# Twenty of the 72 blocks made ahead as split halves, expert numbers written whole, a tile's numbers turned later: a decoder block on one core

## The chip, the core and the metric

The kernel runs on one core of a Trainium2 chip. The metric is the device time of one execution in microseconds (us); lower is better. The core's engines work side by side, each through its own instructions in order: TensorE (PE; its weight loads are PEld), VectorE (DVE), ScalarE (ACT), GpSimd (POOL) and SyncE (SP), which here only issues DMA transfers.

## The reference

One decoder block on 512 tokens of width 1024, in float32:

```python
h = rms_norm(x, norm1_g);  proj = h @ w_in
y_a = hgrn2_mixer(...);  y_b = dilated_attention_mixer(...)
x = x + (sigmoid(ga) * (y_a @ w_branch_a) + sigmoid(gb) * (y_b @ w_branch_b)) @ w_out
x = x + peer_ffn(rms_norm(x, norm2_g), peer_wq, peer_subkeys, peer_u, peer_v)
```

`peer_ffn` has 16384 experts. Each of 8 heads scores two tables of 128 keys, takes the best 16 of each, and of their sums the best 16; an expert's number is 128 times the first key's index plus the second's. A token's 128 experts give `gelu(u[expert] . x) * gate`, with which the rows `v[expert]` are summed.

## The kernel before

The tokens are four tiles of 128. A first "front" (mixers, projections, queries) runs for tile 0, a second for tiles 1 to 3. The experts are then computed in two ways at once.

*By rows.* For the first product tiles 0 and 3 (`UG`), and for the second product tile 3, fetch the chosen rows of `u` or `v` one by one with indirect DMAs from POOL (`row`, L642, into the tiles `rq`, `rowx` and `row`) and sum them on DVE (L661, L684). The list of rows is `idx`, 32-bit integers.

*By blocks.* For tiles 1 and 2 (`UD`, 256 tokens) every one of the 128 blocks of 128 experts is multiplied (`hidden`, L811): the block `ub` comes over SP's queue, TensorE multiplies it with the tokens into `ph` in PSUM, and ACT writes the GELU of it to `pre` (L829; from block 56 on the same thing is written into tiles that are called `rq` and `keys_sb`). For tiles 1, 2 and 0 (`VD`) the second product goes by blocks as well, with the gates as a dense matrix `Gc`. That matrix is made by `scatter_steps`: from a token's expert numbers in two parts (`pk`, first and second key) and its weights (`pkw`), DVE writes `e1` and `e2` (both `e` in the rows, L704 and L707), ACT or DVE `eg` (L711, L713), TensorE multiplies them (`pg`, L718) and ACT writes `Gx` (L719). A step is 16 tokens: 16 products `pg`, in four groups.

The stage "ahead" (L842) makes the first 72 blocks (`NPRE`) before the main loop, since the gates of the dense tiles aren't there yet. Here `hidden` multiplies whole float32 blocks with the whole tokens `h32` (eight products, 16 instructions on TensorE). In the main loop it first splits a block: `halves` (L97) lets ACT write a rounded part `uh` and DVE the rest `ul`, both in a buffer of their own (`bufs=1`), and TensorE makes `uh` by `hH`, `uh` by `hL` and `ul` by `hH`, 24 products. In the stage ahead run also the routing of tile 3, and that of tiles 1 and 2, called when block 12 and block 30 come up (`ROUTE1`, `ROUTE2`); a routing's scatter steps are added to a pump that gives one step at every second block, and another pump gives 0.6 rows of tile 3 a block. A row's DMA and its sum wait for the GELU of the block they were called behind.

A routing (L549) takes top 16 on DVE, and then for each head `eq` (DVE, L597), `sel` and its halving (POOL, L599 and L601) and a sum that leaves the 16 expert numbers (DVE, L602):

```python
nc.vector.tensor_reduce(out=idf[:, n], in_=..., axis=AX.X, op=ALU.add)
if T in UG:
    nc.vector.tensor_copy(idx[:, UG.index(T), hn], idf[:, n])
...
nc.vector.tensor_copy(full[:, hs], idff)
```

At its end (L616 on), for a tile in `VD`, the numbers in `full` are taken apart on DVE into `i12` (its tile is called `ssb`), turned by TensorE (L624) and written to `pk`; the gates are turned by L627 to `pkw`. The main loop has for each of the 128 blocks 18 products (`acc`, L883) of `vh`, `vl` with `ah`, `al`, which ACT and DVE split from a block of `v` and from the gates, and makes blocks 72 to 127 of `hidden` on its way.

A scheduler sets the order of each engine's instructions from the order of the program, the waits and its own model of times; the engines then follow that order.

Of the kernel before, what the change touches and what calls it, by code (L numbers as in the profile page):

```python
# [8 lines left out]
F32 = mybir.dt.float32  # L9
# [5 lines left out]
ALU = mybir.AluOpType  # L15
AX = mybir.AxisListType
PSUM = bass.MemoryType.PSUM

P = 128
# [10 lines left out]
TOPK = 16  # L30
# [9 lines left out]
UG = (0, 3)  # L40
UD = (1, 2)
VD = (1, 2, 0)
# [8 lines left out]

NPRE, RING = 72, 56

ROUTE1, ROUTE2, SCAT_H = 12, 30, 2

GS = 4
ACTW = {0: (0, 4, 8, 12), 1: (0, 4, 8, 12), 2: (4, 12)}
# [16 lines left out]
def kernel(ctx: ExitStack, tc: tile.TileContext, x, wst, par, cst, cols, g2, keys, u, v, ut, vr, out):  # L74
    nc = tc.nc
# [470 lines left out]
        pt = pvg.tile([P, 512], F32, name="vg") if T and bank[0] % 2 else pr.tile([P, 512], F32, name="pr")  # L546
        return pt.rearrange("p (n k) -> p n k", k=NKEY)

    def routing(T, rq):  # L549


        gate = gates[:, T]
        full = rt.tile([P, P], F32, name="full")
        sv = rt.tile([P, PH, TOPK], F32, name="sv")
        for b in range(0, PH, 4):
            tv = rt.tile([P, 4, 2, TOPK], F32, name="tv")
            ti = rt.tile([P, 4, 2, TOPK], U32, name="ti")
            for f in range(2):
                pt = route_bank(T)
                for n in range(4):  # L560
                    nc.tensor.matmul(pt[:, n], rq[64 * f:64 * f + 64, b + n],
                                     keys_sb[64 * f:64 * f + 64, b + n], start=True, stop=True)
                ssb = rt.tile([P, 4, NKEY], F32, name="ssb")
                nc.scalar.activation(ssb, pt, AF.Copy)
                for n in range(4):
                    top16(tv[:, n, f], ti[:, n, f], ssb[:, n])
            tf = rt.tile([P, 4, 2, TOPK], F32, name="tf")
            nc.vector.tensor_copy(tf, ti)
            nc.vector.tensor_scalar(tf[:, :, 0], tf[:, :, 0], float(NKEY), None, op0=ALU.mult)
            cs = rt.tile([P, 4, NCAND], F32, name="cs")  # L570
            ci = rt.tile([P, 4, NCAND], F32, name="ci")
            for src, dst in ((tv, cs), (tf, ci)):
                off = a = 0
                while a < TOPK:
                    n = RUNS[a]
                    e = a
                    while e < TOPK and RUNS[e] == n:
                        e += 1
                    r = e - a
                    o = dst[:, :, off:off + r * n].rearrange("p h (r n) -> p h r n", n=n)  # L580
                    nc.vector.tensor_tensor(out=o, in0=src[:, :, 1, None, :n].to_broadcast([P, 4, r, n]),
                                            in1=src[:, :, 0, a:e, None].to_broadcast([P, 4, r, n]), op=ALU.add)
                    off += r * n
                    a = e
            svb = sv[:, b:b + 4]
            si = rt.tile([P, 4, TOPK], U32, name="si")
            sf = rt.tile([P, 4, TOPK], BF16, name="sf")
            idf = rt.tile([P, 4, TOPK], F32, name="idf")
            shp = [P, NCAND, TOPK]
            by_few = lambda t: t.rearrange("p c (a b) -> p c a b", b=GS)  # L590
            for n in range(4):
                top16(svb[:, n], si[:, n], cs[:, n])
            nc.vector.tensor_copy(sf, si)
            for n in range(4):
                eq = rt.tile(shp, BF16, name="eq")
                sel = rt.tile(shp, F32, name="sel", bufs=2)
                nc.vector.tensor_tensor(out=by_few(eq), in0=iota[:, :NCAND, None, :].to_broadcast([P, NCAND, TOPK // GS, GS]),  # L597
                                        in1=by_few(sf[:, n, None, :].to_broadcast(shp)), op=ALU.is_equal)
                nc.gpsimd.tensor_tensor(out=sel, in0=eq, in1=ci[:, n, :, None].to_broadcast(shp), op=ALU.mult)  # L599
                hc = NCAND // 2  # L600
                nc.gpsimd.tensor_add(sel[:, :hc], sel[:, :hc], sel[:, hc:])  # L601
                nc.vector.tensor_reduce(out=idf[:, n], in_=sel[:, :hc].rearrange("p c k -> p k c"), axis=AX.X, op=ALU.add)  # L602
                if T in UG:
                    hn = slice((b + n) * TOPK, (b + n + 1) * TOPK)
                    nc.vector.tensor_copy(idx[:, UG.index(T), hn], idf[:, n])
            hs = slice(b * TOPK, (b + 4) * TOPK)
            idff = idf.rearrange("p h k -> p (h k)")
            nc.vector.tensor_copy(full[:, hs], idff)
        gt = gate.rearrange("p (h k) -> p h k", k=TOPK)
        gs = rt.tile([P, 2, PH], F32, name="gs")  # L610
        nc.vector.tensor_tensor(out=gt, in0=sv, in1=sv[:, :, 0:1].to_broadcast([P, PH, TOPK]), op=ALU.subtract)
        nc.scalar.activation(gt, gt, AF.Exp)
        nc.vector.tensor_reduce(out=gs[:, 0], in_=gt, axis=AX.X, op=ALU.add)
        nc.vector.reciprocal(gs[:, 1], gs[:, 0])
        nc.vector.tensor_tensor(out=gt, in0=gt, in1=gs[:, 1, :, None].to_broadcast([P, PH, TOPK]), op=ALU.mult)
        if T in VD:  # L616
            pt = route_bank(T)
            i12 = rt.tile([P, 4, NKEY], F32, name="ssb")

            nc.vector.tensor_scalar(i12[:, 0], full, 1.0 / NKEY, -63.5 / NKEY, op0=ALU.mult, op1=ALU.add)  # L620
            nc.vector.tensor_scalar(i12[:, 0], i12[:, 0], RND, RND, op0=ALU.add, op1=ALU.subtract)
            nc.vector.scalar_tensor_tensor(i12[:, 1], i12[:, 0], -float(NKEY), full, op0=ALU.mult, op1=ALU.add)
            for j in range(2):
                nc.tensor.transpose(pt[:, 1 + j], i12[:, j], ident)  # L624
            nc.vector.tensor_copy(pk[:, VD.index(T), 0:2], pt[:, 1:3])
            if T in UD:
                nc.tensor.transpose(pt[:, 3], gate, ident)  # L627
                nc.vector.tensor_copy(pkw[:, VD.index(T)], pt[:, 3])

# [114 lines left out]
    rows, scat = Pump(), Pump()  # L746
# [30 lines left out]
    idx = gat.tile([P, len(UG), P], I32, name="idx", bufs=1)  # L777
# [8 lines left out]
    rt = rctx.enter_context(tc.tile_pool(name="rt", bufs=1, side="left", **TILE))  # L786
# [5 lines left out]

    f = Front(tuple(range(1, 4)), True, background)
    routing(0, rq0)
    rows.add(u_steps(UG[0]))
    mixers(f)
    rows(2 * P)
    rq1, rq2, rq3 = f.post()
# [12 lines left out]
    def hidden(b, pool):  # L811
        if RING <= b < NPRE:

            if (b - RING) % 4 == 0:
                pre4[0] = rq_pool.tile([P, 4, NU], F32, name="rq") if b - RING < 12 else rq_pool.tile([P, 4, NU], F32, name="keys_sb", bufs=1)
            dst = pre4[0][:, (b - RING) % 4]
        else:
            dst = dp.tile([P, NU], F32, name="pre", bufs=RING)
        pre.append(dst)
        ub = us.tile([P, KC, P], F32, name="ub")  # L820
        nc.sync.dma_start(out=ub, in_=ut[b].rearrange("p (k i) -> p k i", k=KC))
        pt = pool.tile([P, NU], F32, name="ph")
        if b < NPRE:

            accumulate(pt, [ub[:, k] for k in range(KC)], h32, slice(None), True)
        else:
            ubs = halves(us.tile([P, KC, P], F32R, name="uh", bufs=1), us.tile([P, KC, P], F32R, name="ul", bufs=1), ub)
            accumulate(pt, [tuple(a[:, k] for a in ubs) for k in range(KC)], (hH, hL), slice(None), True)
        return nc.scalar.activation(dst, pt, AF.Gelu)  # L829

    with tc.tile_pool(name="hw", bufs=1, side="right", **TILE) as hw, \
            tc.tile_pool(name="gb", bufs=1, side="left", **TILE) as gb, \
            tc.tile_pool(name="php", bufs=3, space=PSUM, side="right") as php, \
            tc.tile_pool(name="pg", bufs=3, space=PSUM, side="right") as pg:
        pg_bank = lambda: pg.tile([P, 512], F32, name="pg")
        h32 = hw.tile([P, KC, NU], F32, name="h32")
        nc.vector.tensor_tensor(out=h32, in0=hH.bitcast(F32), in1=hL.bitcast(F32), op=ALU.add)
        scat.add(scatter_steps(0, pg_bank))
        routing(3, rq3)
        rows.add(u_steps(3))  # L840
        lag[0] = 1
        for b in range(NPRE):  # L842
            if b == ROUTE1:
                routing(1, rq1)
                scat.add(scatter_steps(1, pg_bank))
            if b == ROUTE2:
                routing(2, rq2)
                scat.add(scatter_steps(2, pg_bank))
            behind[:] = [hidden(b, php)]
            rows(ROWS_H)  # L850
            if b % SCAT_H == 0:
                scat(1)
        scat(P)
# [103 lines left out]
```

## Time and profile before

| | |
|---|---|
| median of three runs | 1765.86 us (1764.51 to 1772.72) |
| the profiled execution | 1764.48 us, of which the span is 1762.6 us |
| TensorE busy | 1627.5 us (92%), mean granted clock 0.967 |
| VectorE busy | 1321.0 us (75%) |
| ScalarE busy | 735.6 us (42%) |
| GpSimd busy | 672.2 us (38%) |
| moved by DMA | 473.42 MB, 269 GB/s on average |

The profile is one execution. A busy share is an average over stages that have different limits, so each stage is looked at by itself. A matmul's recorded time is longer than the distance to the next one, as they overlap: how fast TensorE goes is read from the distance of the starts, or from the time of a row that merges many.

### The profile page before, as it was taken

Reading aid. Unit: us, or ns where it says so; the run is one execution under the profiler, and the core shown is the slowest. Engines: PE = TensorE matmul, PEld = TensorE weight load, DVE = VectorE, ACT = ScalarE, POOL = GpSimd, SP = SyncE. Lnnn points to the kernel's source line nnn. Section 1 sums busy time; section 2 is a strip of 40 time slices with the busy share of each in tenths; the row PEclk is TensorE's granted clock in tenths of the full one; section 3 lists DMA queues with packets and bytes.
Section 4 is the critical chain, followed back from the end, with each engine's and each line's share of the span. In section 5 each row is a group of like instructions: output and inputs, shape, how many; then the busy total and the mean of one; then the engine's idle time right before and its main releaser. Section 6 shows DMA issues by size and latency. Waiting matters only on the chain.

```text
span 1762.6 us, 26949 instructions
## 1 busy us (share of the span) xinstructions
PE 1627.5 (92%) x9725; PEld 1437.8 (82%) x9725; DVE 1321.0 (75%) x2773; ACT 735.6 (42%) x1411; POOL 672.2 (38%) x502
## 2 busy tenths in 40 slices
PE   7998969789978798998999989999999999999997
PEld 7887969678868797787889977888888878888886
DVE  2113999998988649987985566878788877887887
ACT  3323443334334556633675543333334333343332
POOL 0000366676542004353442224433344454454452
PEclk9999979889989899998999989999999999999999
DMA  8777368879885336575667789999899999898888
GB/s 290 233 231 239 120 225 281 267 275 321 308 305 199 120 120 223 175 248 162 226 223 247 262 268 341 328 321 341 323 326 344 335 322 337 323 333 314 304 303 281
DMA packets 173813, 473.42 MB, mean 269 GB/s; under 512 B 14832, under 2 KB 62192, under 8 KB 173680
## 3 DMA queue, kind: packets, MB, share of 16 engines
q1 hardware_dynamic: 116272, 268.47, 44.6%
q0 software_dynamic: 55296, 201.35, 32.0%
q10 hardware_dynamic: 2112, 1.88, 0.3%
q8 instruction: 77, 1.26, 0.3%
q14 instruction: 56, 0.46, 0.1%
HBM read 442.80 MB, written 27.79 MB: 267 GB/s over the span
## 4 chain that ended last, share of the span: by engine, by line
PE 45%; DVE 22%; DMA 20%; issue 7%; POOL 3%; ACT 2%; DVEq 0%; ACTq 0%; POOLq 0%; SPq 0%
PE acc L883 16%; PE pp L112 15%; PE ph L112 10%; DMA Gc<-g_d 8%; DMA w<-in_wst_dram 3%; DVE e L704 2%; PE pg L718 2%; DVE rq L661 2%; DVE h2g L684 2%; DMA row<-in_u_dram,idx 2%; DMA rowx<-in_u_dram,idx 2%; DMA row<-in_v_dram,idx 1%; DVE wl L99 1%; DVE row L661 1%; DMA rowx<-in_v_dram,idx 1%
## 5 line engine op out<-in xcount | busy, mean ns | idle before, releaser
L112 PE MATMUL ph<-h,ub 128*128 128x256 f32 x1152 | 263.7, 384 | 0.5 <-ACT pre L829 0.5
L883 PE MATMUL acc<-vl,ah 128*128 128x512 f32 x768 | 240.9, 395 | 8.7 <-DVE vl L879 8.7
L112 PEld LDWEIGHTS ph<-h,ub 128*128 128x128 f32 x1152 | 216.7, 193 | 29.4 <-ACT pre L829 0.9
L883 PE MATMUL acc<-vh,al 128*128 128x512 f32 x768 | 239.0, 392 | 0.0
L883 PE MATMUL acc<-vh,ah 128*128 128x512 f32 x768 | 221.1, 392 | 3.8 <-ACT vh L877 3.8
L642 POOL DMA_INDIRECT rowx<-in_u_dram,idx x96 | 131.9, 1374 | 227.7 <-ACT pre L829 56.8
L642 POOL DMA_INDIRECT rowx<-in_v_dram,idx x96 | 148.3, 1545 | 158.5 <-DVE h2g L684 65.8
L98 ACT ACTIVATE ah<-Gc 128x384 fp32r<-128x384 f32 x128 | 67.0, 524 | 309.0 <-PE acc L883 303.7
L883 PEld LDWEIGHTS acc<-vl,ah 128*128 128x128 f32 x768 | 142.7, 189 | 43.4 <-DVE vl L879 14.4
L883 PEld LDWEIGHTS acc<-vh,al 128*128 128x128 f32 x768 | 145.2, 189 | 31.5
L883 PEld LDWEIGHTS acc<-vh,ah 128*128 128x128 f32 x768 | 139.6, 188 | 30.0 <-ACT vh L877 4.4
L879 DVE TENSOR_TENSOR vl<-vb,vh 128x1024 fp32r<-128x1024 f32 x128 | 156.3, 1221 | 9.0 <-ACT vh L877 8.4
L877 ACT ACTIVATE vh<-vb 128x1024 fp32r<-128x1024 f32 x128 | 135.9, 1062 | 57.4 <-DMA vb<-in_vr_dram 56.6
L642 POOL DMA_INDIRECT rq<-in_u_dram,idx x96 | 120.2, 1252 | 88.7 <-DVE rq L661 52.1
L98 ACT ACTIVATE wh<-w 128x512 fp32r<-128x512 f32 x144 | 88.8, 628 | 132.6 <-PE pp L112 60.0
L661 DVE SCALAR_TENSOR_TENSOR rowx<-rowx,h2g 128x1024 f32<-128x1024 f32 x96 | 120.1, 1253 | 30.3 <-DMA rowx<-in_u_dram,idx 19.6
L661 DVE SCALAR_TENSOR_TENSOR rq<-rq,h2g 128x1024 f32<-128x1024 f32 x96 | 131.2, 1370 | 15.0 <-DMA rq<-in_u_dram,idx 15.0
L112 PE MATMUL ph<-hH,ul 128*128 128x256 f32 x448 | 128.4, 287 | 8.8 <-DVE ul L99 8.8
L684 DVE SCALAR_TENSOR_TENSOR h2g<-rowx,hid,h2g 128x1024 f32<-128x1024 f32 x95 | 121.7, 1281 | 18.5 <-DMA rowx<-in_v_dram,idx 18.4
L112 PE MATMUL ph<-hH,uh 128*128 128x256 f32 x448 | 128.1, 286 | 3.7 <-ACT pre L829 3.7
L112 PE MATMUL ph<-hL,uh 128*128 128x256 f32 x448 | 128.1, 286 | 0.0
L719 ACT ACTIVATE Gx<-pg 128x512 f32<-128x512 f32 x96 | 98.2, 1057 | 66.0 <-PE pg L718 59.2
(289 smaller groups left out, 3635.8 us busy)
## 6 DMA issues: line engine op xcount, KB each, us to landing
ub<-in_ut_dram SPq DMA_DIRECT2D x128, 512.0 KB
vb<-in_vr_dram SPq DMA_DIRECT2D x128, 512.0 KB
w<-in_wst_dram SPq DMA_DIRECT2D x107, 512.0 KB
g_d<-Gx SPq DMA_DIRECT2D x24, 960.0 KB
Gc<-g_d SPq DMA_DIRECT2D x15, 1536.0 KB
wh<-in_wst_dram SPq DMA_DIRECT2D x37, 256.0 KB
wl<-in_wst_dram SPq DMA_DIRECT2D x33, 256.0 KB
pairB<-in_x_dram SPq DMA_DIRECT2D x5, 512.0 KB
```

The source lines that it names most:

```text
L98: nc.scalar.activation(hi, x, AF.Copy)
L99: (eng or nc.vector).tensor_tensor(out=lo, in0=x, in1=hi.bitcast(F32), op=ALU.subtract)
L112: nc.tensor.matmul(out, l, r, start=(k == 0 and i == 0), stop=(k == last and i == len(ops) - 1))
L642: d = nc.gpsimd.indirect_dma_start(out=r, out_offset=None, in_=src, in_offset=bass.IndirectOffsetOnAxis(ap=index, axis=0))
L661: d = nc.vector.scalar_tensor_tensor(r, r, 1.0, h2g[T], op0=ALU.mult, op1=ALU.mult, accum_out=hid[:, g, jr:jr + 1])
L684: nc.vector.scalar_tensor_tensor(acc, r, hid[:, g, j:j + 1], acc, op0=ALU.mult, op1=ALU.add)
L704: nc.vector.tensor_tensor(out=e1, in0=iota[:, None, :, 0].to_broadcast(by_token), in1=pk[:, ti, 0, tk, None].to_broadcast(by_token), op=AL ...
L718: nc.tensor.matmul(pt[:, q], e1[:, q0 + q], eg[:, q0 + q], start=True, stop=True)
L719: nc.scalar.activation(Gx[:, :, k + q0:k + q0 + 4].rearrange("p i t -> p t i"), pt, AF.Copy)
L877: behind[:] = [nc.scalar.activation(vH, vb, AF.Copy)]
L879: nc.vector.tensor_tensor(out=vL, in0=vb, in1=vH.bitcast(F32), op=ALU.subtract)
L883: nc.tensor.matmul(acc[t][c], l.rearrange("p g t -> p (g t)")[:, t * P:(t + 1) * P], r[:, c * 512:(c + 1) * 512], start=(b == 0 and i == 0 ...
```

## The change

- `hidden` takes whole blocks only up to `NWHOLE = 52`; blocks 52 to 71 of the stage ahead go in halves, as those of the main loop do.
- The sum over `sel` writes straight to `idx` (tiles 0 and 3) or to `full` (tiles 1 and 2). `full` is copied from `idx` for tile 0 alone; for tile 3 it isn't made.
- The routing of tiles 1 and 2 is called at blocks 10 and 28. What takes the numbers apart and turns them is a function of its own, called at blocks 16 and 34 (`TURN = 6`), and the scatter steps of the tile are added then.

```diff
-ROUTE1, ROUTE2, SCAT_H = 12, 30, 2
+NWHOLE = 52
+ROUTE1, ROUTE2, SCAT_H = 10, 28, 2
+TURN = 6
...
-                nc.vector.tensor_reduce(out=idf[:, n], in_=sel[:, :hc].rearrange("p c k -> p k c"), axis=AX.X, op=ALU.add)
-                if T in UG:
-                    hn = slice((b + n) * TOPK, (b + n + 1) * TOPK)
-                    nc.vector.tensor_copy(idx[:, UG.index(T), hn], idf[:, n])
-            hs = slice(b * TOPK, (b + 4) * TOPK)
-            idff = idf.rearrange("p h k -> p (h k)")
-            nc.vector.tensor_copy(full[:, hs], idff)
+                hn = slice((b + n) * TOPK, (b + n + 1) * TOPK)
+                with nc.allow_low_precision(reason="one of the summands is not zero"):
+                    nc.vector.tensor_reduce(out=idx[:, UG.index(T), hn] if T in UG else full[:, hn],
+                                            in_=sel[:, :hc].rearrange("p c k -> p k c"), axis=AX.X, op=ALU.add)
+            if T in UG and T in VD:
+                hs = slice(b * TOPK, (b + 4) * TOPK)
+                nc.vector.tensor_copy(full[:, hs], idx[:, UG.index(T), hs])
...
-        if T in VD:
+        def numbers():
...
+        if T in VD:
+            if not later:
+                return numbers()
+            return numbers
...
-        if b < NPRE:
+        if b < NWHOLE:
             accumulate(pt, [ub[:, k] for k in range(KC)], h32, slice(None), True)
         else:
...
-            if b == ROUTE1:
-                routing(1, rq1)
-                scat.add(scatter_steps(1, pg_bank))
-            if b == ROUTE2:
-                routing(2, rq2)
-                scat.add(scatter_steps(2, pg_bank))
+            for T, rq, at in ((1, rq1, ROUTE1), (2, rq2, ROUTE2)):
+                if b == at:
+                    turn_numbers = routing(T, rq, True)
+                if b == at + TURN:
+                    turn_numbers()
+                    scat.add(scatter_steps(T, pg_bank))
```

How the scheduler's order moves. First TensorE around the turning of tile 1's numbers, before (`ph<-h_6014,ub` are products of whole blocks, eight a block; `ssb` holds the numbers):

```order
L112 MATMUL ph<-h_6014,ub 128x256 x20
L561 MATMUL vg<-keys_sb,rq 128x128 x4
L112 MATMUL ph<-h_6014,ub 128x256 x61
L624 MATMUL pr<-ident,ssb 128x128
L112 MATMUL ph<-h_6014,ub 128x256
```

and the same place now:

```order
L116 MATMUL ph<-h_6004,ub 128x256 x19
L565 MATMUL vg<-keys_sb,rq 128x128 x4
L116 MATMUL ph<-h_6004,ub 128x256 x45
L628 MATMUL pr<-ident,ssb 128x128
L116 MATMUL ph<-h_6004,ub 128x256 x2
```

Between the routing's last scores and the transpose stand 45 products now, 61 before; counted from the stage's first block, the transpose stands after 229 products of whole blocks now, and after 237 before.

Next TensorE where the last scatter products stand now; behind the last row shown there are 243 more products of halves and then the first `acc`:

```order
L116 MATMUL ph<-hL,uh 128x256
L726 MATMUL pg<-eg,e_9027 128x128
L116 MATMUL ph<-hH,ul 128x256
L726 MATMUL pg<-eg,e_9027 128x128
L116 MATMUL ph<-hH,uh 128x256
L116 MATMUL ph<-hL,uh 128x256
```

The last product of the scatter stands ahead of block 62, ten blocks before the main loop. Before, the last eight stood behind all 72 whole blocks and two blocks in halves.

Last, ScalarE at the same place now (`uh` is the rounded half of a block; the GELUs go to `rq`):

```order
L727 ACTIVATE Gx<-pg 128x4x128 x2
L102 ACTIVATE uh<-ub 128x1024
L837 ACTIVATE rq<-ph 128x256
L102 ACTIVATE ah<-Gc 128x384 x2
L102 ACTIVATE uh<-ub 128x1024
L837 ACTIVATE rq<-ph 128x256
L885 ACTIVATE vh<-vb 128x1024 x2
L102 ACTIVATE uh<-ub 128x1024
L837 ACTIVATE rq<-ph 128x256
L102 ACTIVATE uh<-ub 128x1024
```

A block's `uh` stands ahead of the GELU of the block before it, and the main loop's first `ah` and `vh` stand among them.

## Rows read from the trace of the kernel before

**Rows 1.** Stretches: length, busy us (instructions) of PE, PEld, DVE, ACT, POOL; clock, DMA share, GB/s.

```profile
640.00:930.00 290.00, 267.18 (x1473) 233.94 (x1472) 255.56 (x950) 165.96 (x395) 115.26 (x95) 0.98 0.59 200
930.00:1049.00 119.00, 112.00 (x651) 102.93 (x650) 64.44 (x116) 60.52 (x123) 24.86 (x22) 0.96 0.74 254
1049.00:1763.00 714.00, 686.74 (x3576) 585.83 (x3574) 568.50 (x730) 263.18 (x361) 311.10 (x211) 0.99 0.91 324
```

**Rows 2.** Shorter stretches: late in the stage ahead, at the seam, early in the main loop.

```profile
980.00:990.00 10.00, 10.00 (x63) 9.20 (x63) 6.04 (x11) 6.30 (x14) 2.19 (x2) 1.00 0.83 277
1030.00:1050.00 20.00, 14.07 (x70) 13.30 (x71) 10.73 (x20) 7.59 (x11) 2.12 (x2) 0.74 0.81 265
1090.00:1110.00 20.00, 16.23 (x79) 13.37 (x80) 14.49 (x26) 5.41 (x7) 5.68 (x5) 1.00 0.86 293
```

**Rows 3.** Timeline: start, us, engine, line, operation [idle before and its releaser].

```profile
930.27 0.38 ACT L829 ACTIVATE pre<-ph 128x256 f32<-128x256 f32 x1
...
1048.81 1.53 PE L883 MATMUL acc<-vh,ah 128*128 128x512 f32 x6
```

**Rows 4.** Timeline, PE: whole blocks in a row, and two products of a block in halves.

```profile
779.76 10.31 PE L112 MATMUL ph<-h,ub 128*128 128x256 f32 x47
...
1054.54 0.28 PE L112 MATMUL ph<-hH,ul 128*128 128x256 f32 x1
...
1056.19 0.28 PE L112 MATMUL ph<-hL,uh 128*128 128x256 f32 x1
```

**Rows 5.** Timeline, block 74 in halves on ACT, DVE and PE.

```profile
1042.21 1.06 ACT L98 ACTIVATE uh<-ub 128x1024 fp32r<-128x1024 f32 x1 [3.82 <-issue]
1043.30 1.22 DVE L99 TENSOR_TENSOR ul<-ub,uh 128x1024 fp32r<-128x1024 f32 x1 [2.87 <-ACT uh L98]
1044.58 0.38 PE L112 MATMUL ph<-hH,ul 128*128 128x256 f32 x1 [0.49 <-DVE ul L99]
...
1045.17 0.41 PE L112 MATMUL ph<-hH,uh 128*128 128x256 f32 x1
1045.38 0.41 PE L112 MATMUL ph<-hL,uh 128*128 128x256 f32 x1
...
1048.88 1.06 ACT L98 ACTIVATE uh<-ub 128x1024 fp32r<-128x1024 f32 x1 [4.00 <-PE ph L112]
```

**Rows 6.** Timeline, half a step of the scatter and a row's sum.

```profile
926.05 1.23 DVE L661 SCALAR_TENSOR_TENSOR rowx<-rowx,h2g 128x1024 f32<-128x1024 f32 x1 [0.28 <-DMA rowx<-in_u_dram,idx]
926.13 1.95 PE L718 MATMUL pg<-eg,e 128*128 128x128 f32 x16
...
927.22 1.95 ACT L719 ACTIVATE Gx<-pg 128x512 f32<-128x512 f32 x2 [1.64 <-PE pg L718]
927.22 0.69 DVE L704 TENSOR_TENSOR e<-iota,pk 128x512 f32<-128x512 bf16 x1
...
927.83 0.68 DVE L713 TENSOR_TENSOR eg<-e,pkw 128x512 f32<-128x512 bf16 x1
...
928.97 1.27 ACT L711 ACTIVATE eg<-e,pkw 128x128 f32<-128x128 bf16 x4
929.03 0.42 DVE L707 TENSOR_TENSOR e<-iota,pk 128x512 bf16<-128x512 bf16 x1
```

**Rows 7.** Lines of the routing: count, shortest/median/longest ns, first and last start.

```profile
L605 DVE CAST idx<-idf x16: 143/162/2140, 215.1 to 735.6; 128x16 int32<-128x16 f32 x16
L608 DVE COPY full<-idf x8: 179/189/282, 250.3 to 906.2; 128x64 f32<-128x64 f32 x8
```

**Rows 8.** Timeline, the end of tile 1's routing.

```profile
800.82 0.83 DVE L602 TENSOR_REDUCE idf<-sel 128x16 f32<-128x400 f32 x1 [1.44 <-POOL sel L601]
...
807.12 0.48 PE L624 MATMUL pr<-ident,ssb 128*128 128x128 f32 x1 [7.18 <-DVE ssb L621]
```

**Rows 9.** Two stretches of the second front, columns as in rows 1.

```profile
200.00:250.00 50.00, 37.71 (x230) 36.31 (x230) 49.43 (x121) 19.45 (x30) 29.58 (x21) 0.83 0.54 179
500.00:550.00 50.00, 37.56 (x240) 32.90 (x240) 42.60 (x85) 20.08 (x33) 22.14 (x19) 0.80 0.83 284
```

More of the change, by code (lines that the diff above doesn't have):

```diff
@@ L547, in route_bank, with routing @@
         return pt.rearrange("p (n k) -> p n k", k=NKEY)
-    def routing(T, rq):
+    def routing(T, rq, later=False):
         gate = gates[:, T]
@@ L587, in routing @@
             sf = rt.tile([P, 4, TOPK], BF16, name="sf")
-            idf = rt.tile([P, 4, TOPK], F32, name="idf")
             shp = [P, NCAND, TOPK]
```

## The prediction

> **What bounds the kernel now.** I read the stretches first, PE and the clock against DVE and ACT. TensorE is busy 94% and 96% in 930 to 1049 us and from there to the end, 92% in 640 to 930 us, where VectorE has 88% [rows 1]. So from the scatter on TensorE sets the time, with VectorE close behind before 930 us. Then the timeline of the last blocks made ahead of the main loop: whole float32 blocks (`ph<-h,ub`), and the scatter's products (`pg`) between them. There TensorE never waits: 980 to 990 us has 10.00 of 10, ACT 6.3, DVE 6.0 [rows 2]. Block 52 begins at the GELU of block 51, at 930.27 us (block 56 is the first whose GELU is called `rq`, and it is the fifth after this one); the main loop's first product is at 1048.81 us [rows 3]. So the part that the change rewrites takes 118.5 us, in which TensorE also made blocks 72 to 74, which belong to the main loop.
>
> **The product itself gets cheaper.** A whole block is 16 instructions on TensorE; 47 of them in a row took 10.31 us, 0.219 each: 3.5 us a block. In halves a block is 24; fourteen steps from 1054.54 to 1056.19 are 0.118 each: 2.8 us [rows 4]. Twenty blocks save 20 x 0.67 = 13.4 us of TensorE's work, all that this part offers.
>
> **The chain gets longer.** A whole block needs nothing but its load. In halves, ScalarE writes `uh`, VectorE writes `ul`, then the products run, and `uh` and `ul` have one buffer each: the next `uh` waits for the last product of the block before. The trace shows this cycle at block 74 [rows 5]: `uh` at 1042.21; `ul` at 1043.30, released by `uh`; third product at 1044.58, released by `ul`; from there 22 products; next `uh` at 1048.88, released by the products. With 0.118 a product this is 2.37 + 22 x 0.118 + 0.1 = 5.1 us. It took 6.67, because from 1045.17 on the products stood 0.21 apart. The granted clock of 1030 to 1050 us, where TensorE was busy 14.07 of 20, is 0.74, against 1.00 where it never waits [rows 2]: for part of the time the lower level, 1.2 GHz instead of 2.4.
>
> *The last ten blocks.* In the order as it is now the scatter's last product stands before block 62, and blocks 62 to 71 follow each other with nothing else on TensorE. Nothing hides the chain: at least 10 x 5.1 = 51, at most 10 x 6.67 = 67 us. I take 58, nearer the lower end: in the measured cycle TensorE came out of a longer stall than this chain has.
>
> *Blocks 52 to 61.* All eight scatter steps of the third tile still lie here (128 of 384 products, 32 groups of four), as before, but within ten blocks instead of twenty. By the rows of one half step [rows 6] ACT has 32 `Gx` at 0.98 (two in 1.95), 16 groups of `eg` at 1.27, 10 `uh` at 1.06 and 10 GELUs at 0.38: 66 us. DVE has 32 times 0.69 + 0.42, 16 `eg` at 0.68, 10 `ul` at 1.22, 6 row sums at 1.23: 66 us. TensorE has 10 x 2.8 for the blocks and 16 half steps at 1.95: 59. So at least 66, now from ACT and DVE; 78 if the two hold each other up by a sixth. I take 72.
>
> Together 72 + 58 = 130 against 118.5: **+11.5**. The three blocks made early before now lie in the main loop, where TensorE is the bound: 3 x 2.8 = **+8.5**.
>
> **What is given back.** After the seam TensorE was busy only 16.23 of 20 us in 1090 to 1110 [rows 2], 3.8 lost, and before it the last scatter groups, the first gates and the first `vh` stood one behind the other. Now these are made under the chain of blocks 62 to 71. A gain of 0 to 6, I take **-3**, since the main loop's DMA share of 0.91 [rows 1] needs no fewer bytes than before.
>
> **Whole numbers.** Sixteen casts go at a median of 0.162 us (one took 2.14), and of eight copies at 0.19 two are left, as casts [rows 7]; each sum over `sel`, 0.83 [rows 8], writes its integers or `full` itself. Neither form of output is in the trace; I bound its change by a cast less and a cast more, 0.16, and take 0, since it reads the same 400 elements. VectorE is nearly full in the stage ahead before 930 us, where half of the casts and four of the copies go: 8 x 0.16 + 6 x 0.19, some **-2**. The first tile's eight casts lie beside the second front, where VectorE is full in 200 to 250 us [rows 9]. Only 1.3 us of work goes there, but its order changes from there on; I take **-2**, with 8 either way.
>
> **The turn.** TensorE waited 7.18 us for tile 1's numbers, whose last sums hang on GpSimd [rows 8]. In the order now the transpose stands after 229 products of whole blocks instead of 237: not later, but one block (3.5 us) earlier, as the routing begins two blocks earlier too. VectorE has one row sum and a dozen casts and copies less ahead of it, some 3 us. So this wait stays: 0, with 4 either way, and 7 gained if the transpose did come late enough. No DMA is added; loads move with their blocks in SP's queue, and each GELU that lets POOL ask for a row comes with its block.
>
> **Sum.** 11.5 + 8.5 - 3 - 2 - 2 = +13, on the profiled execution's 1764.48: 1777.5, so **1778 us**. That execution lies 1.4 below the median of the runs, 1765.86, which is small beside the bounds; a difference under 0.5% (8.8 us) can't be told from none here.
>
> **Rivals.** *1. The second front closes its gaps: faster.* VectorE is full or nearly so there, and TensorE is busy for only 37.71 and 37.56 of 50 us in 200 to 250 and 500 to 550 us [rows 9]: 24.7 us lost while row sums and routing stand among the front's own work on VectorE. The new order places them anew. From 22 us gained there it is faster by over 0.5% in spite of the tail: 1778 - 22 = 1756 us. For it: the order does change, from the first direct sum on. Against: some 2 us of work are gone, and one gap closed alone leaves it within 0.5%. Chance 0.18.
>
> *2. ACT and DVE keep up: no difference to be told.* Blocks 52 to 61 in 66 us and the last ten in 51, at the full clock: the tail is 117, -1.5 + 8.5 - 3 - 2 - 2 = 0, 1765 us. For it: under whole blocks DVE and ACT were busy 6 of 10, so there is room to run ahead. Against: one buffer each, and both lower bounds at once. It decides below a tail of 126. Chance 0.33.
>
> *3. The clock falls in the whole chain.* In blocks 62 to 71 TensorE would work 2.8 of each 5.1 us, 55%, and in 1030 to 1050 us 70% came with a clock of 0.74 [rows 2]. Then the last ten take 67 and the ten before 78: tail 145, 26.5 + 8.5 - 1 = +34, 1798 us. Against: that stretch is one seam. Chance 0.12. The Trainium skill, "TensorE: Matmul & The Clock Gate", section "A second HAM failure mode: psum-queue depth-cycling", says that short idles between groups of products, if frequent, make the clock swing between its two levels, at a cost that comes back with every burst. By that rule, the trace agrees for one cycle, 6.67 against 5.1 us; no run here shows ten in a row.
>
> *4. The turn comes late enough after all.* The change would then do what its words say, and 7 us are gained: 1771 us, within rival 2's bounds and in its chance. The order speaks against it.
>
> **Chances.** My forecast (1774 to 1790) 0.37, rival 1 0.18, rival 2 0.33, rival 3 0.12. So faster by over 0.5%: 0.18; within: 0.33; slower: 0.49. The forecast's own range is 1774 to 1790; for 8 in 10 it takes in rival 2 and the nearer parts of rivals 1 and 3: 1754 to 1799.
>
> **What would show it.** Right: in blocks 62 to 71 the products release each `uh`, 5.1 to 6.7 us apart, with TensorE idle or at a lower clock there; 125 to 135 us from the GELU of block 51 to the first main product; the rest from there 4 to 6 us longer. Wrong: `uh` less than 4.5 us apart, TensorE 94% busy up to the main loop, or a difference made before 640 us that is larger than the tail's.

## The result and the profile after

The changed kernel takes **1821.38 us** (median; 1817.37 to 1825.38) against 1767.99 of the kernel before, run beside it: ratio 1.0294, 95% interval 1.0254 to 1.0333. Slower, as forecast, but by 53 us where 12 were forecast, and above the range.

The two profiled executions in stages, cut at the first GELU of the stage ahead, the GELUs of blocks 51, 61 and 71, and the first and last `acc`:

| stage, us | before | after | change | forecast |
|---|---|---|---|---|
| up to the first GELU ahead | 653.2 | 664.0 | +10.8 | -2 |
| blocks 1 to 51 ahead | 277.1 | 278.7 | +1.6 | -2 |
| blocks 52 to 61 | 47.0 | 73.2 | | |
| blocks 62 to 71 | 47.0 | 71.2 | | |
| from there to the first `acc` | 24.5 | 0.5 | | |
| these three, the tail | 118.5 | 144.9 | +26.4 | +11.5 |
| first to last `acc` | 707.1 | 724.8 | +17.7 | +5.5 |
| rest | 6.7 | 5.7 | -1.0 | 0 |
| span | 1762.6 | 1818.1 | +55.5 | +13 |

Each column is one execution. Others with whole blocks (runs 2 to 4 below) have 660.6 to 663.7 us in the first row and 698.4 to 702.0 in the main loop, so a single stage is known to some 10 us only. The run that differs from the changed kernel by the halves alone (run 2) is the better measure: tail +30.8, main loop +26.4, front +0.3.

The rows of the changed kernel that answer to [rows 1, 3]. Stretches: length, busy us (instructions) of PE, PEld, DVE, ACT, POOL; clock, DMA share, GB/s.

```profile
943.00:1016.00 73.00, 63.32 (x483) 59.81 (x482) 57.55 (x100) 59.35 (x113) 10.97 (x14) 0.98 0.66 236
1016.00:1040.00 24.00, 15.87 (x68) 14.57 (x69) 14.14 (x26) 5.70 (x9) 4.06 (x2) 0.61 0.93 304
1040.00:1087.00 47.00, 33.79 (x174) 30.63 (x172) 13.16 (x15) 10.18 (x15) 7.99 (x6) 0.77 0.41 140
1087.00:1300.00 213.00, 194.08 (x1001) 166.08 (x1001) 153.86 (x234) 72.98 (x101) 75.51 (x60) 0.95 0.86 296
1300.00:1812.00 512.00, 501.92 (x2646) 429.47 (x2645) 413.36 (x491) 192.37 (x266) 224.23 (x151) 1.00 0.91 324
```

Two things are new: in the last ten blocks TensorE is busy 49.7 of 71 us at a granted clock of 0.61 and 0.77; and the first 213 us of the main loop have TensorE idle for 19 us and the clock at 0.95. From 1300 us on TensorE is busy 98%.

One block of the last ten in the timeline of the changed kernel, which answers to [rows 5] (start, us, engine, line, operation [idle before and its releaser]):

```profile
1059.41 1.06 ACT L102 ACTIVATE uh<-ub 128x1024 fp32r<-128x1024 f32 x1 [5.35 <-PE ph L116]
...
1060.49 1.23 DVE L103 TENSOR_TENSOR ul<-ub,uh 128x1024 fp32r<-128x1024 f32 x1 [4.31 <-ACT uh L102]
...
1061.77 0.39 PE L116 MATMUL ph<-hH,ul 128*128 128x256 f32 x1 [0.76 <-DVE ul L103]
...
1063.03 0.41 PE L116 MATMUL ph<-hH,ul 128*128 128x256 f32 x1
1063.24 0.41 PE L116 MATMUL ph<-hH,uh 128*128 128x256 f32 x1
...
1066.08 1.06 ACT L102 ACTIVATE uh<-ub 128x1024 fp32r<-128x1024 f32 x1 [5.35 <-PE ph L116]
```

It is the chain of [rows 5] link by link: `uh`, then `ul` 1.08 later, then the products, 0.21 apart for most of the block, and the next `uh` after 6.67 us, released by the products. Blocks 67 to 71 all take 6.67 or 6.68.

What holds the main loop up stands on VectorE (run 9 tests it). Its timeline in the changed kernel:

```profile
1126.68 0.55 DVE L103 TENSOR_TENSOR al<-Gc,ah 128x384 fp32r<-128x384 f32 x1
1127.15 1.21 DVE L887 TENSOR_TENSOR vl<-vb,vh 128x1024 fp32r<-128x1024 f32 x1
1137.48 2.77 DVE L880 TENSOR_TENSOR Gc<-pre,Gc 128x256 f32<-128x256 f32 x8 [9.11 <-DMA Gc<-g_d]
...
1142.92 1.22 DVE L887 TENSOR_TENSOR vl<-vb,vh 128x1024 fp32r<-128x1024 f32 x1
...
1191.99 2.77 DVE L880 TENSOR_TENSOR Gc<-pre,Gc 128x256 f32<-128x256 f32 x8 [10.15 <-DMA Gc<-g_d]
...
1239.71 2.77 DVE L880 TENSOR_TENSOR Gc<-pre,Gc 128x256 f32<-128x256 f32 x8 [5.85 <-DMA Gc<-g_d]
...
1335.11 2.77 DVE L880 TENSOR_TENSOR Gc<-pre,Gc 128x256 f32<-128x256 f32 x8 [3.21 <-DMA Gc<-g_d]
```

and TensorE's row at that place, in the same kernel:

```profile
1144.19 1.22 PE L891 MATMUL acc<-vl,ah 128*128 128x512 f32 x2 [6.76 <-DVE vl L887]
```

The dense gates `Gc` come in 16 groups of eight blocks, all but the first over SP's queue (L876), into two alternating buffers; for each group eight multiplies with `pre` (L880) stand together in VectorE's order. Here they come up at once after block 8's `vl`, wait 9.11 us for the load, and the next `vl` stands behind them, done at 1144.14. TensorE has run out by then and waits 6.76 us for it.

The same multiplies in the kernel before:

```profile
1098.77 2.77 DVE L872 TENSOR_TENSOR Gc<-pre,Gc 128x256 f32<-128x256 f32 x8 [5.51 <-DMA Gc<-g_d]
1138.19 2.77 DVE L872 TENSOR_TENSOR Gc<-pre,Gc 128x256 f32<-128x256 f32 x8 [1.53 <-DMA Gc<-g_d]
1181.00 2.77 DVE L872 TENSOR_TENSOR Gc<-pre,Gc 128x256 f32<-128x256 f32 x8 [2.78 <-DMA Gc<-g_d]
```

The issues of the third group's load, in the changed kernel and before:

```profile
1120.69 0.52 SPq L876 DMA_DIRECT2D Gc<-g_d  x1
```

```profile
1080.96 0.53 SPq L868 DMA_DIRECT2D Gc<-g_d  x1
```

From the issue to the multiply it is 16.8 us in the changed kernel and 17.8 before, so the load takes about as long. What differs is how soon VectorE stands there waiting: 7.7 us after the issue now, 12.3 before. The order shows why. Before, the multiplies of the third, fourth and fifth group stand behind 10, 18 and 26 `al`; now behind 9, 17 and 25: one block less of work on VectorE between a load and its use. For the third to the sixth group, all one block early, VectorE comes 7.4 to 10.0 us after the issue and waits 5.9 to 10.2; before, 12.3 to 13.8 and 1.5 to 5.5. The seventh group (the row at 1335.11) stands behind 42 `al` in both kernels: in the changed one VectorE comes 12.7 us after the issue and waits 3.2.

### The profile page after: what moved, and what is told of

The parts are those of the page before. It is cut to its first block, busy times and chain, and to the rows that moved or that the text cites. A ratio compares the mean times of both kernels' runs of the same rounds, so it can differ in the third digit from the quotient of the medians.

```text
span 1818.1 us, 27338 instructions
## 1 busy us (share of the span) xinstructions
PE 1649.3 (91%) x9885; PEld 1457.4 (80%) x9885; DVE 1341.1 (74%) x2771; ACT 757.1 (42%) x1432; POOL 651.6 (36%) x502
## 4 chain that ended last, share of the span: by engine, by line
PE 37%; DVE 24%; DMA 24%; issue 10%; POOL 3%; ACT 2%; DVEq 0%; POOLq 0%; SPq 0%; ACTq 0%
PE pp L116 13%; PE acc L891 13%; PE ph L116 7%; DMA Gc<-g_d 6%; DMA w<-in_wst_dram 4%; DMA rq<-in_u_dram,idx 3%; DMA rowx<-in_v_dram,idx 3%; DMA rowx<-in_u_dram,idx 2%; DVE e L712 2%; DVE rowx L669 2%; PE pg L726 2%; DVE rq L669 2%; DMA vb<-in_vr_dram 2%; DVE row L669 1%; DVE h2g L692 1%
## 5 line engine op out<-in xcount | busy, mean ns | idle before, releaser
L891 PE MATMUL acc<-vl,ah 128*128 128x512 f32 x768 | 243.1, 398 | 26.3 <-DVE vl L887 26.3
L891 PE MATMUL acc<-vh,ah 128*128 128x512 f32 x768 | 225.0, 392 | 0.2 <-ACT vh L885 0.2
L650 POOL DMA_INDIRECT rowx<-in_u_dram,idx x96 | 121.0, 1260 | 261.9 <-ACT vh L885 79.2
L116 PE MATMUL ph<-hH,uh 128*128 128x256 f32 x608 | 180.1, 296 | 14.4 <-ACT uh L102 14.3
L891 PEld LDWEIGHTS acc<-vl,ah 128*128 128x128 f32 x768 | 144.4, 191 | 60.8 <-DVE vl L887 30.9
L116 PE MATMUL ph<-h,ub 128*128 128x256 f32 x832 | 190.9, 386 | 0.0
L116 PE MATMUL ph<-hH,ul 128*128 128x256 f32 x608 | 180.6, 297 | 11.1 <-DVE ul L103 11.1
L116 PE MATMUL ph<-hL,uh 128*128 128x256 f32 x608 | 178.1, 293 | 0.0
L116 PEld LDWEIGHTS ph<-h,ub 128*128 128x128 f32 x832 | 158.1, 194 | 21.4
L669 DVE SCALAR_TENSOR_TENSOR rq<-rq,h2g 128x1024 f32<-128x1024 f32 x96 | 123.8, 1297 | 23.6 <-DMA rq<-in_u_dram,idx 23.3
L116 PEld LDWEIGHTS ph<-hH,uh 128*128 128x128 f32 x608 | 122.0, 201 | 20.4 <-ACT uh L102 17.1
L116 PEld LDWEIGHTS ph<-hH,ul 128*128 128x128 f32 x608 | 122.3, 201 | 14.7 <-DVE ul L103 13.7
```

The costliest lines, as they stand in the source:

```text
L116: nc.tensor.matmul(out, l, r, start=(k == 0 and i == 0), stop=(k == last and i == len(ops) - 1))
L650: d = nc.gpsimd.indirect_dma_start(out=r, out_offset=None, in_=src, in_offset=bass.IndirectOffsetOnAxis(ap=index, axis=0))
L669: d = nc.vector.scalar_tensor_tensor(r, r, 1.0, h2g[T], op0=ALU.mult, op1=ALU.mult, accum_out=hid[:, g, jr:jr + 1])
L891: nc.tensor.matmul(acc[t][c], l.rearrange("p g t -> p (g t)")[:, t * P:(t + 1) * P], r[:, c * 512:(c + 1) * 512], start=(b == 0 and i == 0 ...
```

## Experiments

All against the kernel before, run beside them; "main loop" is from the first to the last `acc`, "`al` ahead" how many stand ahead of the third group's multiplies in VectorE's order, "`vl`" TensorE's waits for `vl` in the main loop. Stages are of one profiled execution each.

| kernel | ratio (95% interval) | first GELU | tail | main loop | `al` ahead | `vl` |
|---|---|---|---|---|---|---|
| before | 1 | 653.2 | 118.5 | 707.1 | 10 | 8.7 |
| changed | 1.0294 (1.0254 to 1.0333) | 664.0 | 144.9 | 724.8 | 9 | 26.3 |
| 1 halves alone | 1.0258 (1.0210 to 1.0306) | 660.8 | 136.9 | 726.2 | 9 | 22.1 |
| 2 no halves | 1.0006 (0.9972 to 1.0039) | 663.7 | 114.1 | 698.4 | 10 | 9.8 |
| 3 direct sums alone | 1.0003 (0.9970 to 1.0036) | 660.8 | 117.0 | 702.0 | 10 | 11.6 |
| 4 turn alone | 1.0004 (0.9977 to 1.0032) | 660.6 | 116.5 | 700.4 | 10 | 10.1 |
| 5 `uh` first | 1.0018 (0.9983 to 1.0053) | 663.4 | 108.5 | 711.3 | 9 | 13.7 |
| 6 two buffers | 0.9974 (0.9941 to 1.0007) | 663.8 | 97.8 | 715.3 | 10 | 19.4 |
| 7 filler | 1.0272 (1.0205 to 1.0339) | 663.6 | 138.3 | 721.2 | 9 | 24.5 |
| 8 last ten only | 1.0176 (1.0106 to 1.0247) | 666.1 | 119.2 | 727.4 | 9 | 23.0 |
| 9 gates held | 1.0105 (1.0032 to 1.0178) | 668.1 | 145.2 | 694.2 | 13 | 5.0 |
| 10 before, gates held | 0.9976 (0.9949 to 1.0003) | 656.4 | 113.8 | 695.0 | 13 | 4.6 |
| 11 two buffers, held | 0.9882 (0.9853 to 0.9912) | 667.9 | 97.7 | 688.3 | 13 | 3.8 |
| 12 the same, `uh` first | 0.9932 (0.9905 to 0.9959) | 662.4 | 102.2 | 701.3 | 13 | 7.6 |

### Which part of the change costs

**1, halves alone.** The kernel before with

```diff
+NWHOLE = 52
...
-        if b < NPRE:
+        if b < NWHOLE:
```

> The kernel before with blocks 52 to 71 in halves and nothing else changed. Theory A (the chain of the halves costs the tail): from the GELU of block 51 to the first main product about 145 us, as in the changed kernel, against 118.5 before; the last blocks 6.7 us apart; the first GELU of the stage ahead within 3 us of the 653.2 of before; a total of 25 to 45 us more than before, depending on whether the main loop also takes its 12 us beyond three more blocks. Theory B (the direct sums and the turn cost more than the halves): the total is under 20 us more than before.

1813.83 us against 1768.99. Theory A at the top of its span: nearly all of the loss, in the tail and the main loop both. Three details were missed: the tail is 136.9 us instead of 145, the first GELU comes at 660.8, and the last blocks came 6.7 us apart in part only: of the last ten four took 5.15 to 6.2 us, six 6.45 to 10.2.

**2, no halves.** The changed kernel with

```diff
-NWHOLE = 52
+NWHOLE = 72
```

> The changed kernel with all 72 blocks ahead whole: direct sums and later turn are kept. Theory A: the tail is back at 118 us and the main loop at 707 us, what is left is the second front, so 5 to 13 us more than before (first GELU of the stage ahead near 664 instead of 653.2). Theory B: 25 us or more above before. A third case, that the second front's 10.8 us come from elsewhere (the scheduler placing the front otherwise because later work is longer): no difference to before.

1770.63 against 1768.99. Tail and main loop come back; the total is not 5 to 13 us above before but equal to it, although the first GELU is at 663.7. Against this kernel, which differs from the changed one by the halves alone, the tail loses 30.8 and the main loop 26.4 us, and the front nothing.

**3, direct sums alone.** The kernel of run 2 with `ROUTE1, ROUTE2 = 12, 30` and `TURN = 0`.

> Direct sums alone; blocks whole, routing at 12 and 30, numbers turned at once. If the new order of VectorE's work in the second front costs its 10.8 us there, the first GELU of the stage ahead is near 664 and the total 8 to 13 us above before. If the casts that are left out count and the order doesn't, 2 to 4 us less than before, the first GELU at or before 653.

1770.13 against 1768.99: neither. The first GELU is at 660.8.

**4, turn alone.** The kernel before with the split of `numbers()`, `ROUTE1, ROUTE2 = 10, 28` and `TURN = 6`.

> The later turn alone, with the routing at 10 and 28 and the numbers turned at 16 and 34. By the forecast 0 with 4 us either way, since the transpose stands one block earlier on TensorE. If the turn comes late enough after all, 7 us less. If the earlier routing takes VectorE's time from the second front's last work, some 3 to 8 us more, with the first GELU of the stage ahead unchanged at 653.

1767.97 against 1768.99: zero, as forecast. Of the wait for tile 1's numbers [rows 8] 3.34 of 7.18 us are left, so the turn does gain some 4 us there; they don't show in the total. And the first GELU, which this edit can't move, is late as well. The rows of ScalarE's timeline in the kernel before, in halves alone and in turn alone, one each:

```profile
653.20 0.39 ACT L829 ACTIVATE pre<-ph 128x256 f32<-128x256 f32 x1
```

```profile
660.75 0.38 ACT L831 ACTIVATE pre<-ph 128x256 f32<-128x256 f32 x1
```

```profile
660.61 0.38 ACT L835 ACTIVATE pre<-ph 128x256 f32<-128x256 f32 x1
```

TensorE and VectorE have the same order up to there in these three. So one and the same front ended 7.5 us apart in different executions, and the profile of before was an early one. The last two, 0.14 us apart, are from one chip; whether the chip makes the difference isn't shown.

### The chain of the halves

**5, `uh` first.** The changed kernel with the products of a block in another order:

```diff
-            accumulate(pt, [tuple(a[:, k] for a in ubs) for k in range(KC)], (hH, hL), slice(None), True)
+            ops = [(ubs[0], h, k) for k in range(KC) for h in (hH, hL)] + [(ubs[1], hH, k) for k in range(KC)]
+            for i, (w, h, k) in enumerate(ops):
+                nc.tensor.matmul(pt, w[:, k], h[:, k], start=(i == 0), stop=(i == len(ops) - 1))
```

> The changed kernel, but a block in halves multiplies all sixteen products of uh first and the eight of ul after them; as much work, another order. If the wait for ul (the third product) and the single buffer of uh are what makes the chain, uh comes free after 16 products instead of 23, and ul is made under the first sixteen: the steady 6.67 us a block of the last ten falls to 3.5 to 5.5, the tail (GELU of block 51 to the first main product, 145 us now) to 118 to 130, the total 15 to 30 us under the changed kernel. If instead loads, ACT or DVE set the pace of the last ten, the cycle stays above 6 and the total within 6 us of the changed kernel.

1773.38 against 1768.54, 48 us under the changed kernel: more than expected. The twenty blocks take 106.7 us instead of 144.4, 5.3 a block on average, with not a product fewer. They aren't even: of the last ten, nine take 2.5 to 6.4 us, and block 71 takes 12.65, with a wait of 7.17 for `uh`. Part of the scatter (80 of its 256 instructions on TensorE in the tail) now lies behind block 61, where the changed kernel has none. The changed kernel's pace was set by the wait for `ul` while `uh` stays taken, not by the loads or by what ACT and DVE have to do.

**6, two buffers.** The changed kernel with

```diff
-            ubs = halves(us.tile([P, KC, P], F32R, name="uh", bufs=1), us.tile([P, KC, P], F32R, name="ul", bufs=1), ub)
+            ubs = halves(us.tile([P, KC, P], F32R, name="uh", bufs=2), us.tile([P, KC, P], F32R, name="ul", bufs=2), ub)
```

> The changed kernel with two buffers each for uh and ul. If the single buffers make the chain, a block's halves are written while the block before is multiplied: the last ten blocks run at TensorE's pace, 2.8 to 4 us each, tail 110 to 125 us, clock at or near 1.00 there, total 20 to 40 us under the changed kernel (part of that in the main loop, if its stall at the gates' loads goes with the order of VectorE). If ACT and DVE are what is short, the tail stays above 135 us.

1760.58 against 1768.54, 61 us under the changed kernel: more than expected, as is the tail of 97.8. Its stretches for blocks 52 to 61, and from there to the first `acc`, columns as above:

```profile
941.00:985.00 44.00, 43.14 (x372) 42.97 (x371) 39.64 (x65) 36.59 (x68) 10.47 (x10) 1.00 0.84 302
985.00:1038.00 53.00, 50.36 (x429) 49.75 (x427) 45.28 (x72) 40.71 (x73) 14.85 (x11) 1.00 0.88 300
```

ACT and DVE do in 97 us what took 144 (ACT 77.3 us of work here and 75.2 there, DVE 84.9 and 84.9), the clock stays at 1.00 in both stretches, and half of the scatter (125 of the 256 instructions) now lies behind block 61. TensorE is busy 93.5 of the 97 us: it sets the pace now. The main loop, though, takes 715.3: it has waits for `vl` (19.4 us) and for `vh` (7.6), the longest of them right behind the gates' multiplies. Yet these stand behind 10 and 19 `al` for the third and fourth group, no earlier than before: that they stand one block early isn't the only thing that makes them wait.

**7, filler.** The changed kernel with work added for blocks 62 to 71 that does nothing for the result:

```diff
+            if 62 <= b < NPRE:
+                for k in range(4):
+                    nc.tensor.matmul(pt, ub[:, k], h32[:, k], start=(k == 0), stop=(k == 3))
             ubs = halves(us.tile([P, KC, P], F32R, name="uh", bufs=1), us.tile([P, KC, P], F32R, name="ul", bufs=1), ub)
```

> The changed kernel with work added: for blocks 62 to 71 TensorE first makes four whole float32 products (eight instructions, 1.75 us) into the same bank, which the halves' first product then overwrites. They need the load alone and fill the time in which TensorE waits for uh and ul. If the lower clock makes the last ten blocks' cycle 6.67 instead of 5.1 us, the products come 0.118 apart again, the granted clock of that stretch is above 0.95 and the cycle is 5.1 to 5.6 us, so the tail 8 to 14 us shorter in spite of 17 us of extra work. If the clock is only a sign and the chain itself takes that long, the cycle stays at 6.7 or grows toward 8.4, the tail is as long or up to 17 us longer.

The stretch from 1040 us to the first `acc`, and one block's products in the timeline:

```profile
1040.00:1079.00 39.00, 31.40 (x205) 28.63 (x205) 11.93 (x14) 9.26 (x14) 7.99 (x6) 0.96 0.47 159
```

```profile
1055.91 1.92 PE L837 MATMUL ph<-h,ub 128*128 128x256 f32 x8
1057.49 0.47 PE L116 MATMUL ph<-hH,ul 128*128 128x256 f32 x1
1057.79 0.28 PE L116 MATMUL ph<-hH,uh 128*128 128x256 f32 x1
1057.91 0.28 PE L116 MATMUL ph<-hL,uh 128*128 128x256 f32 x1
```

In TensorE's order the filler stands between the second and the third product of a block, so it fills the wait for `ul`; the wait for `uh` stays (1.03 us ahead of this block). With more to do TensorE is through sooner: the last ten blocks take 63.9 us instead of 71.2, the products are 0.12 apart, the clock is 0.96 instead of 0.77. The cycle is 5.9 us in three blocks in a row (5.16 to 6.29 in the last six), not 5.1 to 5.6: the filler lasts 0.7 us longer than `ul` does (`ul` ends at 1056.78, its product starts at 1057.49). The gain in the tail, 6.6 us where 8 to 14 were expected, is too small to be told in the total: 1.0272 of before, and the changed kernel 1.0294, with intervals that overlap.

**8, last ten only.** The changed kernel with `NWHOLE = 62`.

> The changed kernel with NWHOLE = 62: only the last ten blocks ahead in halves. If each ten blocks cost by themselves (73.2 us and 71.2 us where ten whole blocks took 47.0), the ten before keep their 47 us, the last ten take 52 to 71, and the tail is 118 to 135 us; with the main loop's stall as in the changed kernel (its gates' multiplies stand as early, behind 9, 17, 25 al's) the total is 20 to 40 us above before. If the loss in the last ten only came from running behind after the ten ahead of them, the tail is within 5 us of 117 and the total within 15 us of before.

Blocks 52 to 61 take 47.0 us, the last ten 71.6, and the tail is 119.2, that of before, since the seam after block 71 (24.5 us before) is gone here as well. Yet the total is 1.0176 of before, some 31 us more, as expected. Of the 33.8 us between the spans (1796.4 against 1762.6) 20.3 lie in the main loop, 12.9 ahead of the first GELU: the main loop's loss is a thing apart from the tail's.

### The main loop

**9, gates held.** The changed kernel with

```diff
-        nc.vector.tensor_mul(gsl[:, :ngu], a.rearrange("p (g t) -> p g t", t=GT), gsl[:, :ngu])
+        m = nc.vector.tensor_mul(gsl[:, :ngu], a.rearrange("p (g t) -> p g t", t=GT), gsl[:, :ngu])
+        if b >= 2 * GB:
+            behind[:] = [vhs[b // GB * GB - 4]]
+            turn(m, "a gate's turn")
...
         behind[:] = [nc.scalar.activation(vH, vb, AF.Copy)]
+        vhs.append(behind[0])
```

> The changed kernel, but from the third group of eight gate blocks on VectorE's eight multiplies of a group (Gc<-pre) may start only after the vh of the block four ahead of that group; in the order they then stand behind 13, 21, 29 al's instead of 9, 17, 25. Theory: in the main loop the changed kernel loses some 16 us more than before because these multiplies stand one block earlier in VectorE's order than before (behind 9 instead of 10 al's, and so on), and wait 9.1, 10.2 and 5.9 us for the gates' load with the next vl queued behind them. If so, those waits fall under 2 us each, the main loop goes from 725 to 705 to 712 us, the total 13 to 20 us under the changed kernel, with the tail unchanged at 145. Rival: the main loop is longer because of its three more blocks and a lower clock; then the total stays within 5 us.

1790.08 against 1768.54: 31 us under the changed kernel. The main loop takes 694.2 us with the same 56 blocks to make. Its rows on VectorE and on TensorE, and for TensorE those of the changed kernel (busy, mean ns of one | idle before and releaser):

```profile
1157.62 0.75 DVE L881 TENSOR_TENSOR Gc<-pre,Gc 128x256 f32<-128x256 f32 x2
1159.44 2.15 DVE L881 TENSOR_TENSOR Gc<-pre,Gc 128x256 f32<-128x256 f32 x6
1200.25 2.76 DVE L881 TENSOR_TENSOR Gc<-pre,Gc 128x256 f32<-128x256 f32 x8
```

```profile
L896 PE MATMUL acc<-vl,ah 128*128 128x512 f32 x768 | 239.3, 393 | 5.0 <-DVE vl L892 4.9
L896 PE MATMUL acc<-vh,al 128*128 128x512 f32 x768 | 238.4, 392 | 0.0
L896 PE MATMUL acc<-vh,ah 128*128 128x512 f32 x768 | 223.0, 391 | 1.0 <-ACT vh L889 1.0
```

```profile
L891 PE MATMUL acc<-vl,ah 128*128 128x512 f32 x768 | 243.1, 398 | 26.3 <-DVE vl L887 26.3
L891 PE MATMUL acc<-vh,al 128*128 128x512 f32 x768 | 240.5, 395 | 0.0
L891 PE MATMUL acc<-vh,ah 128*128 128x512 f32 x768 | 225.0, 392 | 0.2 <-ACT vh L885 0.2
```

From the third group on no wait for a load stands ahead of the multiplies any more. Of the 30.6 us 21.3 are waits for `vl`, and 7.9 the products themselves (708.6 to 700.7 us busy). The stretch after the seam shows why those got shorter:

```profile
1092.00:1300.00 208.00, 205.59 (x1095) 176.46 (x1094) 169.21 (x257) 79.59 (x110) 91.25 (x67) 1.00 0.94 332
```

The granted clock is 1.00 where it was 0.95: the long stalls had also cost clock. The tail is unchanged, 145.2. Theory right as far as the waits go, size (13 to 20 us) too small; since the multiplies moved by four blocks, not by one, the run doesn't price the one block by itself.

**10, before with gates held.** The same edit in the kernel before.

> The kernel before with the gates' multiplies held as in the run before (from the third group on, until the vh of the block four ahead of the group), all else as it was. Theory: the kernel before loses time at the same place, 62 to 67 us of VectorE's waits for the gates' loads over the main loop with the next vl queued behind them, and some 14 us of TensorE's. Its main loop goes from 700 to 707 to about 692 to 697, so 6 to 13 us less in all. Rival: what was won by holding in the changed kernel was only the damage of its seam; then the total is within 4 us of before.

The main loop is 695.0 us, as expected; the total, 1760.48 against 1765.49, can't be told from before with certainty. So the kernel before had such stalls too: its main loop is 12.1 us shorter without them, though its waits for `vh` rise from 3.8 to 9.2 us.

**11, two buffers and gates held.** Both edits in the changed kernel.

> The changed kernel with two buffers each for uh and ul and with the gates' multiplies held. If the two losses are separate, tail about 98 us as with two buffers alone, main loop 694 to 703 instead of 715, total 12 to 20 us under two buffers alone, so about 1740 to 1750 and faster than both kernels. If the main loop is bound by TensorE's own work there, less than 6 us under two buffers alone.

**1746.58 us against 1765.49**, faster than both kernels: 0.9882 of before, with the whole interval below 1. The tail is that of two buffers (97.7), the main loop 688.3: the two losses were separate. Its stretches around the first `acc` (at 1043.9 us), hardly anything idle and no clock lost:

```profile
987.00:1032.00 45.00, 45.00 (x391) 45.00 (x390) 39.56 (x63) 38.79 (x70) 15.22 (x12) 1.00 0.81 282
1032.00:1250.00 218.00, 214.08 (x1137) 183.43 (x1136) 176.05 (x272) 86.70 (x120) 86.41 (x64) 1.00 0.95 341
```

**12, the same with `uh` first.**

> The same with all products of uh ahead of those of ul. With two buffers the wait for ul is hidden by the block before, so no difference to two buffers with held gates (within 4 us); if ul is late even so (VectorE has the row sums and al, vl in front of it), 4 to 10 us less, from shorter waits for ul in blocks 52 to 71.

1755.25 against 1746.58 of the run beside it: 8.7 us slower, where none or a gain was expected. Tail (+4.5) and main loop (+13.0, with 3.8 more waiting for `vl` and 4.6 more for `vh`) both lose; why wasn't followed up.

## Why the prediction was wrong

The sign was right, and the mechanism that it put first, the chain, was at work. Two terms of its sum failed, 58 for the last ten blocks and -3 given back in the main loop, the second for a reason that it had not looked at.

- **Blocks 52 to 61, "I take 72": 73.2.** Right in size, in part by luck. The bound of 66 us of work on ACT and DVE didn't hold: they are busy 59 and 58 of 73 us, and TensorE 63, its longer waits (7.2 us) all for the scatter's `eg`. How much the single buffers add in these ten blocks isn't shown by itself: the 44.3 us of two buffers are less work, since half of the scatter lies behind block 61 there.
- **The last ten, "I take 58, nearer the lower end": 71.2.** This step failed. The argument was that the cycle of 6.67 us [rows 5] came out of a longer stall than this chain has. It holds for this chain too: 6.67 for the last five, and 7.7 to 9.9 for blocks 62 to 64, ahead of which the first gates' multiplies, `ah` and `vh` stand on VectorE and ScalarE; so even the upper bound, 67, was too low. In 1016 to 1087 us TensorE waits 22.1 us for `uh` and `ul`; its 240 products take the other 49, 0.204 each, where 0.118 [rows 4] would make 28. So the clock costs as much as the wait: the granted clock is 0.61 and then 0.77, the lower level, 1.2 GHz, for more and then for less than half of the time. Rival 3 had this mechanism at a chance of 0.12. Its tail of 145 is met by luck (78 + 67 for 73.2 + 71.2), and its +34 gives back only 1, where the forecast's own terms give back 7: with those it is +28, 1792 us. By the rule of the Trainium skill that stood beside rival 3 ("TensorE: Matmul & The Clock Gate", "A second HAM failure mode: psum-queue depth-cycling"), frequent short idles make the clock swing; the trace agrees, now ten blocks in a row, and the filler, which fills the wait for `ul`, brings 0.77 to 0.96.
- **The main loop, "+8.5" and "given back -3": +17.7.** The +8.5 holds: three more blocks it is (56 made behind the first `acc`, 53 before), and TensorE is busy 9.7 us longer. The -3 is the second failed step: the idle time rises by 8. In the main loop before:

```profile
L883 PE MATMUL acc<-vl,ah 128*128 128x512 f32 x768 | 240.9, 395 | 8.7 <-DVE vl L879 8.7
L883 PE MATMUL acc<-vh,ah 128*128 128x512 f32 x768 | 221.1, 392 | 3.8 <-ACT vh L877 3.8
L112 PE MATMUL ph<-hH,ul 128*128 128x256 f32 x425 | 120.4, 283 | 8.3 <-DVE ul L99 8.3
```

In the changed kernel the waits for `vh` and `ul` are 0.2 and 2.2 us, 9.7 less, but those for `vl` are 26.3, 17.6 more; 18.7 of the 26.3 are four waits right behind the four groups of multiplies that stand one block early. The prediction took the 3.8 us lost in 1090 to 1110 us [rows 2] for the seam's. Most of it (1.87 us of waiting for `vh` and 1.32 for `vl`, at 1101 and 1104) falls where ScalarE and VectorE stand for loads, VectorE 5.51 us for the third group's gates (the row at 1098.77); such a loss can grow with the order, and did. VectorE's order against the gates' loads was not read. Of the loss against the kernel without halves, 26.4 us, the waits for `vl` are the larger part (26.3 against 9.8); held, the loop takes 694.2.
- **Whole numbers -4, turn 0: no difference that can be told.** Both alone are within 0.4% of before. Rivals 1 and 4 fall as mechanisms for the total: the second front closed no gaps, and of the turn's 7 us some 4 came. The front's 10.8 us in the two profiles don't belong to the change as far as the totals go: the kernel without halves has the late front (663.7) and before's time, though its profile also has a shorter tail and main loop than before's. That direct sums make the front some us longer stays possible: 660.8 to 668.1 in the ten profiles with them, 653.2 to 660.8 in the four without, on several chips. In the prediction's sum, "four of the copies" and "6 x 0.19" don't agree; either makes some 2 us.
- **What the change offers, 13.4 us: there, once the chain is gone.** With two buffers the tail is 97.8 against 114.1 with whole blocks, with one block more made in it. Another order alone brings 108.5. Rival 2 (ACT and DVE keep up) is what two buffers make true.

## What to carry to other kernels

Cheaper products behind a longer chain only pay where the chain is hidden, here by a second buffer for what it hands on or, in part, by an order of the products that needs the late half last. Take the cycle as measured, clock and all, and don't assume that the next one will do better. And where a change moves the seam to the next stage, read the order there as well: an instruction that waits for a load holds up all that is queued behind it. Hold it back to where its load has landed: that was worth 31 us in the changed kernel.

## What was not expected

- More work made a stretch shorter: eight added instructions a block took the cycle from 6.67 to 5.9 us, with the granted clock up from 0.77 to 0.96.
- The same order of TensorE's and VectorE's instructions ended the front 7.5 us apart in different executions (653.2, 660.6, 660.8), so a difference of that size between two single profiles there says nothing of a change.
- A stall of TensorE for VectorE costs more than its own length: holding the gates back saved 21.3 us of waits and 7.9 us of the same products' busy time.
